# Zero-padded 128-row products in the retention loop, and the 128-row products of a block's outputs put first in the rwkv stage

## The chip, the cores and the metric

The kernel runs on one core of a Trainium2 chip. The metric is the device time of one execution in microseconds, as the median of several runs. Five engines work side by side, each through its own instructions in a fixed order: PE (TensorE, matrix products; PEld is its loading of the stationary operand), DVE (VectorE), ACT (ScalarE), POOL (GpSimd) and SP (SyncE, which issues DMAs here). SBUF is the on-chip memory of 128 rows (partitions); products land in PSUM.

## What is computed

Two blocks of a network run one after the other over 256 tokens of width 1024 in float32. The first block holds a bidirectional retention with 8 heads (64 wide for q and k, 128 for v), a Fourier branch, a gated merge and a convolutional feed-forward part. The second holds an RWKV-7 time mixing with 8 heads of 64, an mLSTM, a gated merge and a PEER layer that fetches 128 expert rows for each token. The parts that the change touches are these:

```python
# retention, first block (o is summed over both directions)
scores = einsum('bhncd,bhnsd->bhncs', qc, kc) * intra_decay
intra = einsum('bhncs,bhnse->bhnce', scores, vc)
inter = einsum('bhncd,nbhde->bhnce', q_dec, s_prev)
o = (intra + inter)
# rwkv, second block
def step(S, inp):
    sa = einsum('bhvk,bhk->bhv', S, -kk_t)
    S = S * w_t[:, :, None, :] + sa[..., None] * b_t[:, :, None, :] + v_t[..., None] * k_t[:, :, None, :]
    return S, einsum('bhvk,bhk->bhv', S, r_t)
```

The kernel computes the retention of all 256 tokens as one chunk: scores times a decay matrix, times v, plus q with a decay times the state `st` that comes from the context. It computes the rwkv recurrence in blocks of 128 tokens, each of two chunks of 64.

## The kernel before

Activations lie transposed, with the width on the 128 rows. A linear layer (`lin`, `lin_units`) streams its float32 weights in units of 512 KB: SP issues the load into one of four buffers `wf`, ACT rounds it to `wh` (line 245), DVE forms the rest `wl` (line 246), three buffers each, and PE makes three products for each 128 rows of contraction (lines 267 to 269 with 256 columns into `psb`, lines 277 to 279 with 512 columns into `psa`).

**The retention loop** (lines 591 to 619) runs over 8 heads. Two heads share the 128 rows of `qt` and `kt`: an even head has rows 0 to 63, an odd one rows 64 to 127 (`rows`). For each head DVE and ACT make the decay matrix `toe` and, for each pair of heads, the decayed q `qd`. Line 606 makes the scores in two halves `pssc`, contracting the head's 64 rows; DVE multiplies them with the decay into `pt` (line 607). Into `pso`, for each of two token blocks, go two products with `v` that contract 128 tokens (line 612) and two with `st` that contract the head's 64 rows (line 614). DVE takes the statistics of the result (lines 617, 618), ACT copies it to `o` (line 619). `st` is filled just before by line 580 (128 rows contracted, 64 outputs in the upper or lower half of the array's columns) and two ACT copies (line 582).

**The outputs of a block in the rwkv stage** (lines 1081 to 1091) follow the chain of the states `zs`. For each of the 8 heads, two products contract 128 tokens (lines 1086 and 1087, 64 outputs), and two contract the head's 64 rows against the states of the two chunks (line 1090, 64 outputs). All go into one PSUM buffer `psy`, and one ACT copy takes it to `yt` (line 1091). This is done twice, for b = 0 and 1.

A float32 product is two passes on PE; in the profile each pass is one instruction, with a load of its own. PSUM has two sets of four buffers; the products here use those of `ps`, the linear layers those of `psd`. Outside the last stage a planner orders each engine's instructions ahead of time, by what is ready and by the order of the program. So products of neighbouring linear layers stand between those of the loop: the gate projection `win[4]`, `win[5]` in the retention loop, `wg2` in the rwkv stage. Named slots for larger tiles come from three size classes, and a freed slot goes to the end of its class's list. The last stage (`experts`) gathers 256 times 1 MB of expert rows by DMAs that POOL issues (line 1472).

Of the kernel before, what the change touches and what calls it, by code (L numbers as in the profile page):

```python
# [19 lines left out]
P = 128  # L20
T = 256
# [3 lines left out]
RH = 8  # L25
# [194 lines left out]
class _Builder:  # L220
# [196 lines left out]
    def block1(self, xt):  # L417
        nc, tc, a, S = self.nc, self.tc, self.a, self.S
# [99 lines left out]
        r = self.rstd(xt)  # L518
# [5 lines left out]
        qt = S([P, 4, T], "qt")  # L524
        f = S([P, 2, 512], "f")

        def fcopy(ps, b):
            nc.scalar.copy(f[:, b], ps)
# [20 lines left out]
        kt = S([P, 4, T], "kt")  # L549
# [15 lines left out]
        v = S([P, 2, D], "v")  # L565
# [8 lines left out]

        st = S([P, 2, 4, P], "st")
        for i in range(2):
            ps = self.ps("psst").rearrange("p (a e) -> p a e", a=4)
            for h in range(RH):
                for b in range(2):
                    nc.tensor.matmul(ps[64 * (h % 2):64 * (h % 2) + 64, h // 2, :], kw[:, i, b, h * 64:(h + 1) * 64],  # L580
                                     vc[:, b, h * P:(h + 1) * P], start=b == 0, stop=b == 1)
            nc.scalar.copy(st[:, i], ps)
        next(rest)
# [7 lines left out]
        for h in range(RH):  # L591
            rows = slice(64 * (h % 2), 64 * (h % 2) + 64)
            if h % 2 == 0:
                qd = self.tmp([P, 2, T], "qd")
# [8 lines left out]
            ps = self.ps("pssc").rearrange("p (a t) -> p a t", a=2)  # L603
            pt = self.tmp([P, 2, T], "pt")
            for j in range(2):
                nc.tensor.matmul(ps[:, j], kt[rows, h // 2, j * P:(j + 1) * P], qt[rows, h // 2, :], start=True, stop=True)
                nc.vector.tensor_mul(pt[:, j], ps[:, j], e[:, 128:384] if j == 0 else e[:, 0:256])
            po = self.ps("pso")
            for b in range(2):
                q = po[:, b * P:(b + 1) * P]  # L610
                for j in range(2):
                    nc.tensor.matmul(q, pt[:, j, b * P:(b + 1) * P], v[:, j, h * P:(h + 1) * P], start=j == 0, stop=False)
                for i in range(2):
                    nc.tensor.matmul(q, qd[rows, i, b * P:(b + 1) * P], st[rows, i, h // 2, :], start=False, stop=i == 1)
            for b in range(2):
# [3 lines left out]
            nc.scalar.copy(o[:, :, h * P:(h + 1) * P], po[:, :256].rearrange("p (b e) -> p b e", b=2))  # L619
        self.dump("o", o)  # L620
        gs = S([P, 2, D], "gs")
        for j in range(2):
# [34 lines left out]

        S.free("v", "kt", "qt", "st")
        rs = cp.tile([P, 2, RH], F32, name="rs8")
# [203 lines left out]
    def rwkv(self, hx, soon, xt, r, C, V):  # L863
# [107 lines left out]
        for b in range(2):  # L971
# [3 lines left out]
            tm = {}  # L975
# [80 lines left out]
            for half in range(2):  # L1056
# [23 lines left out]
                yield  # L1080
            ps = self.ps("psy").rearrange("p (n t) -> p n t", n=4)
            for h in range(RH):
                rows = slice(64 * (h % 2), 64 * (h % 2) + 64)
                hs = slice(h * 64, (h + 1) * 64)
                n = h // 2
                nc.tensor.matmul(ps[rows, n], tm["v"][:, hs], mt(h, 3), start=True, stop=False)
                nc.tensor.matmul(ps[rows, n], u[:, hs], mt(h, 1), start=False, stop=False)
                for half in range(2):
                    tr = slice(64 * half, 64 * half + 64)
                    nc.tensor.matmul(ps[rows, n, tr], zs[2 * b + half][rows, n], kr[rows, n, b, 1, tr], start=False, stop=half == 1)  # L1090
            nc.scalar.copy(yt[:, :, bs], ps)
            S.free("tmz0", *(("tmz1",) if b == 0 else ()), "tmv", "tmq", "rt", "tt", "ktt", "u", "uv")
# [512 lines left out]
```

## Time and profile before

| | |
|---|---|
| median of 3 runs | 1519.98 us (1519.15 to 1525.84) |
| profiled execution | 1517.43 us, its span 1515.7 us |
| PE busy | 1350.3 us (89%) |
| DVE busy | 1047.1 us (69%) |
| ACT busy | 737.7 us (49%) |
| POOL busy | 295.2 us (19%) |
| retention loop | 144.9 to 194.4 us |
| outputs of the two blocks in the rwkv stage | 676.3 to 684.2 and 754.6 to 762.7 us |
| gathering of expert rows | from about 850 us to the end |

The profile is taken from one execution. In the rows of the next section, a product's tile is written as rows contracted times outputs (`64*128` is 64 rows and 128 outputs), then the shape of the moving operand; `x4` means that four such instructions are merged in one row. A product's length holds its way through the array, so that products overlap each other: what counts is the step from one start to the next.

### The profile page before, as it was taken

Reading aid. Unit: us, or ns where it says so; the run is one execution under the profiler, and the core shown is the slowest. Engines: PE = TensorE matmul, PEld = TensorE weight load, DVE = VectorE, ACT = ScalarE, POOL = GpSimd, SP = SyncE. Lnnn points to the kernel's source line nnn. Section 1 sums busy time; section 2 is a strip of 40 time slices with the busy share of each in tenths; the row PEclk is TensorE's granted clock in tenths of the full one; section 3 lists DMA queues with packets and bytes.
Section 4 is the critical chain, followed back from the end, with each engine's and each line's share of the span. In section 5 each row is a group of like instructions: output and inputs, shape, how many; then the busy total and the mean of one; then the engine's idle time right before and its main releaser. Section 6 shows DMA issues by size and latency. Waiting matters only on the chain.

```text
span 1515.7 us, 21089 instructions
## 1 busy us (share of the span) xinstructions
PE 1350.3 (89%) x7496; PEld 969.3 (64%) x7496; DVE 1047.1 (69%) x2095; ACT 737.7 (49%) x1561; POOL 295.2 (19%) x277
## 2 busy tenths in 40 slices
PE   6999999989999999999999779877987798777776
PEld 2788699989999988899889525333532253222222
DVE  6774676867777688755468778678567775867544
ACT  7633454456555586534465454443534444434433
POOL 0000000000000000000000254443444345444331
PEclk9999999999999999999999999999999999999999
DMA  8655376645555444312138599999999999999995
GB/s 289 234 177 176 122 236 214 223 156 186 187 182 183 165 148 133 112 57 84 57 129 282 224 422 419 421 421 421 405 422 421 421 408 422 421 422 420 422 421 237
DMA packets 76568, 413.07 MB, mean 273 GB/s; under 512 B 8640, under 2 KB 8768, under 8 KB 43312
## 3 DMA queue, kind: packets, MB, share of 16 engines
q0 software_dynamic: 38880, 276.59, 44.2%
q1 hardware_dynamic: 37440, 134.88, 26.7%
q8 instruction: 59, 0.97, 0.3%
q14 instruction: 45, 0.37, 0.1%
q10 hardware_dynamic: 144, 0.26, 0.0%
HBM read 410.66 MB, written 1.05 MB: 272 GB/s over the span
## 4 chain that ended last, share of the span: by engine, by line
PE 50%; DMA 19%; DVE 12%; issue 11%; POOL 5%; ACT 4%; POOLq 0%; DVEq 0%; SPq 0%; ACTq 0%
DMA uv<-in_uv_dram,rows 18%; PE psb L267 8%; PE psb L268 8%; PE psb L269 8%; POOL uv L1472 5%; DVE uv L1479 4%; PE acc L1485 2%; PE psa L277 2%; PE psa L279 2%; PE psa L278 2%; PE acc L267 1%; PE acc L269 1%; PE acc L268 1%; ACT wh L245 1%; PE psr L1032 1%
## 5 line engine op out<-in xcount | busy, mean ns | idle before, releaser
L1485 PE MATMUL acc<-uv,dg 128*128 128x512 f32 x1024 | 488.5, 614 | 131.3 <-ACT dg L1483 128.8
L1485 PEld LDWEIGHTS acc<-uv,dg 128*128 128x128 f32 x1024 | 182.1, 191 | 426.7 <-ACT dg L1483 268.2
L1479 DVE CUSTOM_DVE_ANT_0 uv<-uv,hn 128x1024 f32<-128x1024 f32 x256 | 310.2, 1222 | 172.8 <-DMA uv<-in_uv_dram,rows 165.9
L1472 POOL DMA_INDIRECT uv<-in_uv_dram,rows x256 | 283.3, 1107 | 396.0 <-PE acc L1485 264.9
L246 DVE TENSOR_TENSOR wl<-wf,wh 128x1024 fp32r<-128x1024 f32 x213 | 258.3, 1218 | 128.3 <-ACT wh L245 126.8
L245 ACT CAST wh<-wf 128x1024 fp32r<-128x1024 f32 x213 | 222.3, 1046 | 240.5 <-PE psb L268 145.7
L267 PE MATMUL psb<-hxh,wh 128*128 128x256 f32 x960 | 279.3, 291 | 4.2 <-ACT hxh L370 3.4
L268 PE MATMUL psb<-hxl,wh 128*128 128x256 f32 x960 | 273.3, 285 | 0.0
L269 PE MATMUL psb<-hxh,wl 128*128 128x256 f32 x960 | 272.7, 285 | 0.2 <-DVE wl L246 0.2
L1480 ACT ACTIVATE act<-act 128x1 f32<-128x1 f32 x256 | 52.1, 203 | 341.2 <-DVE act L1479 341.1
L267 PEld LDWEIGHTS psb<-hxh,wh 128*128 128x128 f32 x960 | 184.2, 192 | 10.7 <-issue 4.7
L268 PEld LDWEIGHTS psb<-hxl,wh 128*128 128x128 f32 x960 | 184.1, 192 | 3.7 <-issue 2.9
L269 PEld LDWEIGHTS psb<-hxh,wl 128*128 128x128 f32 x960 | 183.8, 192 | 1.0 <-issue 0.3
L1483 ACT ACTIVATE dg<-io,act 128x128 f32<-128x128 f32 x256 | 103.3, 403 | 8.3
L1481 ACT ACTIVATE act<-act,gate 128x1 f32<-128x1 f32 x256 | 76.0, 297 | 8.3
L970 POOL MEMSET mt<- 128x2048 f32 x2 | 3.5, 1804 | 350.8 <-PE psb L268 350.8
L833 POOL DMA_DIRECT2D wq<-in_wq_dram x12 | 6.3, 531 | 260.7 <-PE pstm L982 141.3
L478 DVE SCALAR_TENSOR_TENSOR macc<-wf,cs,macc 128x512 f32<-128x512 f32 x56 | 42.0, 749 | 19.1 <-DMA wf<-in_wmod_dram 18.3
L267 PE MATMUL acc<-fh,wh 128*128 128x256 f32 x176 | 49.5, 281 | 0.0
L268 PE MATMUL acc<-fl,wh 128*128 128x256 f32 x176 | 49.4, 281 | 0.0
L269 PE MATMUL acc<-fh,wl 128*128 128x256 f32 x176 | 49.4, 281 | 0.0
L277 PE MATMUL psa<-wh,hxh 128*128 128x512 f32 x96 | 38.4, 400 | 0.0
(463 smaller groups left out, 2071.2 us busy)
## 6 DMA issues: line engine op xcount, KB each, us to landing
wf<-in_wmod_dram SPq DMA_DIRECT2D x48, 512.0 KB, 4.2
wf<-in_wup_dram SPq DMA_DIRECT2D x44, 512.0 KB, 3.5
wf<-in_win_dram SPq DMA_DIRECT2D x28, 512.0 KB, 4.5
wf<-in_wdn_dram SPq DMA_DIRECT2D x22, 512.0 KB, 3.7
wf<-in_wbg_dram SPq DMA_DIRECT2D x16, 512.0 KB, 4.5
wf<-in_wo_dram SPq DMA_DIRECT2D x16, 512.0 KB, 4.8
wf<-in_wml_dram SPq DMA_DIRECT2D x16, 512.0 KB, 3.4
wf<-in_wg_dram SPq DMA_DIRECT2D x16, 512.0 KB, 3.4
```

Of the source, the lines that this page charges most:

```text
L245: self.nc.scalar.copy(h, src)
L246: self.nc.vector.tensor_sub(l, src, h.bitcast(F32))
L267: nc.tensor.matmul(ps, p, xh[:, k0 + k, :], start=s, stop=False, skip_group_check=True)
L268: nc.tensor.matmul(ps, p, xl[:, k0 + k, :], start=False, stop=False, skip_group_check=True)
L269: nc.tensor.matmul(ps, q, xh[:, k0 + k, :], start=False, stop=e, skip_group_check=True)
L277: nc.tensor.matmul(ps, x, wh[:, k, :n], start=s, stop=False)
L1472: nc.gpsimd.indirect_dma_start(t, None, a["uv"], bass.IndirectOffsetOnAxis(ap=self.rows[b][:, h, k:k + 1], axis=0))
L1479: nc.vector.tensor_tensor_reduce(t[:, :D], t[:, :D], hn[:, b], 1.0, 0.0, ALU.mult, ALU.add, act)
L1480: nc.scalar.activation(act, act, AF.Gelu)
L1481: nc.scalar.activation(act, act, AF.Copy, scale=self.gate[b][:, h, k:k + 1])
L1483: nc.scalar.activation(dg, ident, AF.Copy, scale=act)
L1485: nc.tensor.matmul(acc[b][c], dg, t[:, D + c * 512:D + (c + 1) * 512], start=False, stop=h == PH - 1 and k == TOPK - 1, skip_group_check=True)
```

## The change

In the retention loop, the 64-row products become 128-row products. `qz` holds two copies of `qt`, one with zeros in the lower 64 rows, the other with zeros in the upper ones; POOL writes the zeros and copies the rest. `st` gets a place for each of the 8 heads, with zeros (written by POOL) in the rows of the other head; four ACT copies fill it instead of two. Lines 606 and 614 then contract all 128 rows. `st` moves to a larger slot class, `qz` takes two slots more, and `v`, `kt`, `qt`, `st` and `qz` are released right after the loop.

In the rwkv stage, two PSUM buffers `py` take the even and the odd heads. The two 128-row products of all 8 heads are issued first, then the 64-row products of all heads. The accumulation is opened by the first product in each buffer and closed by the last. Two ACT copies take the two halves to `yt`.

```diff
+        qz = [S([P, 4, T], "qz%d" % i) for i in range(2)]
+        nc.gpsimd.memset(qz[0][64:], 0.0)
+        nc.gpsimd.memset(qz[1][:64], 0.0)
...
-        st = S([P, 2, 4, P], "st")
+        st = S([P, 2, RH, P], "st")
+        nc.gpsimd.memset(st[64:, :, ::2], 0.0)
+        nc.gpsimd.memset(st[:64, :, 1::2], 0.0)
+        for i in range(2):
+            r = slice(64 * i, 64 * i + 64)
+            nc.gpsimd.tensor_copy(qz[i][r], qt[r])
...
-            nc.scalar.copy(st[:, i], ps)
+            for b in range(2):
+                r = slice(64 * b, 64 * b + 64)
+                nc.scalar.copy(st[r, i, b::2], ps[r])
...
-            rows = slice(64 * (h % 2), 64 * (h % 2) + 64)
...
-                nc.tensor.matmul(ps[:, j], kt[rows, h // 2, j * P:(j + 1) * P], qt[rows, h // 2, :], start=True, stop=True)
+                nc.tensor.matmul(ps[:, j], kt[:, h // 2, j * P:(j + 1) * P], qz[h % 2][:, h // 2, :], start=True, stop=True)
...
-                    nc.tensor.matmul(q, qd[rows, i, b * P:(b + 1) * P], st[rows, i, h // 2, :], start=False, stop=i == 1)
+                    nc.tensor.matmul(q, qd[:, i, b * P:(b + 1) * P], st[:, i, h], start=False, stop=i == 1)
...
+        S.free("v", "kt", "qt", "st", "qz0", "qz1")
...
-        S.free("v", "kt", "qt", "st")
...
-            ps = self.ps("psy").rearrange("p (n t) -> p n t", n=4)
+            py = [self.ps("psy").rearrange("p (n t) -> p n t", n=4) for _ in range(2)]
+            at2 = lambda h: (slice(64 * (h % 2), 64 * (h % 2) + 64), h // 2, slice(h * 64, (h + 1) * 64))
             for h in range(RH):
-                rows = slice(64 * (h % 2), 64 * (h % 2) + 64)
-                hs = slice(h * 64, (h + 1) * 64)
-                n = h // 2
-                nc.tensor.matmul(ps[rows, n], tm["v"][:, hs], mt(h, 3), start=True, stop=False)
-                nc.tensor.matmul(ps[rows, n], u[:, hs], mt(h, 1), start=False, stop=False)
+                rows, n, hs = at2(h)
+                nc.tensor.matmul(py[h % 2][rows, n], tm["v"][:, hs], mt(h, 3), start=n == 0, stop=False, skip_group_check=True)
+                nc.tensor.matmul(py[h % 2][rows, n], u[:, hs], mt(h, 1), start=False, stop=False, skip_group_check=True)
+            for h in range(RH):
+                rows, n, hs = at2(h)
                 for half in range(2):
                     tr = slice(64 * half, 64 * half + 64)
-                    nc.tensor.matmul(ps[rows, n, tr], zs[2 * b + half][rows, n], kr[rows, n, b, 1, tr], start=False, stop=half == 1)
-            nc.scalar.copy(yt[:, :, bs], ps)
+                    nc.tensor.matmul(py[h % 2][rows, n, tr], zs[2 * b + half][rows, n], kr[rows, n, b, 1, tr], start=False,
+                                     stop=n == 3 and half == 1, skip_group_check=True)
+            for i in range(2):
+                rows = at2(i)[0]
+                nc.scalar.copy(yt[rows, :, bs], py[i][rows])
```

## Rows read from the trace of the kernel before

**Rows 1.** The page, part 1: busy time, share of span, instructions

```profile
PE 1350.3 (89%) x7496; PEld 969.3 (64%) x7496; DVE 1047.1 (69%) x2095; ACT 737.7 (49%) x1561; POOL 295.2 (19%) x277
```

**Rows 2.** Busy time by stage: retention loop, and the fetching of expert rows

```profile
core 0: us, PE busy (x) PEld busy (x) DVE busy (x) ACT busy (x) POOL busy (x), PEclk, DMA share, GB/s
144.90:194.40 49.50, 49.50 (x235) 34.52 (x235) 32.64 (x94) 18.76 (x31) 1.83 (x3) 1.00 0.40 132
...
849.00:1505.00 656.00, 524.49 (x1368) 223.50 (x1366) 451.63 (x1052) 286.19 (x860) 283.31 (x256) 0.99 1.00 412
```

**Rows 3.** Timeline of PE and PEld, retention loop: start, length, engine, line, operands

```profile
144.89 0.70 PE L606 MATMUL pssc<-qt,kt 64*128 64x256 f32 x2
...
162.22 0.52 PEld L614 LDWEIGHTS pso<-st,qd 64*128 64x128 f32 x4
162.22 0.71 PE L614 MATMUL pso<-st,qd 64*128 64x128 f32 x4
162.86 0.71 PE L612 MATMUL pso<-v,pt 128*128 128x128 f32 x4
163.50 0.71 PE L614 MATMUL pso<-st,qd 64*128 64x128 f32 x4
...
192.41 0.50 PE L277 MATMUL psa<-wh,hxh 128*128 128x512 f32 x1
192.74 0.39 PE L278 MATMUL psa<-wl,hxh 128*128 128x512 f32 x1
192.97 0.40 PE L279 MATMUL psa<-wh,hxl 128*128 128x512 f32 x1
```

**Rows 4.** PE's groups by line and form, 144.89 to 192.4: busy, mean

```profile
L612 PE MATMUL pso<-v,pt 128*128 128x128 f32 x64 | 12.7, 300 | 0.0
L614 PE MATMUL pso<-st,qd 64*128 64x128 f32 x64 | 11.3, 297 | 0.0
L606 PE MATMUL pssc<-qt,kt 64*128 64x256 f32 x32 | 11.1, 428 | 0.0
L279 PE MATMUL psa<-wh,hxl 128*128 128x512 f32 x19 | 8.2, 432 | 0.0
...
L482 PE MATMUL pst<-io,macc 128*128 128x1 f32 x9 | 1.2, 241 | 0.0
```

**Rows 5.** Waits, 144.9 to 194.4: us in total, times, longest

```profile
DVE bs L617 <- PE pso L614: 10.0, 8, 2.4
...
DVE pt L607 <- PE pssc L606: 3.2, 6, 1.5
```

**Rows 6.** PE's timeline in the rwkv stage, one head of block b = 1

```profile
755.60 0.43 PE L1086 MATMUL psy<-mt,tmv 128*64 128x128 f32 x2
...
756.18 0.44 PE L1090 MATMUL psy<-kr,zs 64*64 64x64 f32 x4
756.55 0.43 PE L1086 MATMUL psy<-mt,tmv 128*64 128x128 f32 x2
```

**Rows 7.** PE's timeline: three runs of products that reach only part of the array

```profile
140.21 3.77 PE L580 MATMUL psst<-vc,kw 128*64 128x128 f32 x64
...
671.17 0.68 PE L1077 MATMUL psz<-tmv,tmz 64*64 64x64 f32 x16
...
747.80 0.68 PE L1067 MATMUL psu<-zs,ktt 64*64 64x64 f32 x8
```

**Rows 8.** Single lines, x count: duration ns min/median/max, first and last start

```profile
L970 POOL MEMSET mt<- x2: 1802/1804/1807, 541.0 to 542.7; 128x2048 f32 x2
...
L413 DVE TENSOR_TENSOR qt<-qt,ru x2: 691/692/693, 71.5 to 73.7; 128x512 f32<-128x512 f32 x2
...
L1091 ACT COPY yt<-psy x2: 587/588/589, 684.3 to 762.8; 128x512 f32<-128x512 f32 x2
```

**Rows 9.** Waits of ACT, 194.4 to 250: us in total, times, longest

```profile
ACT wh L245 <- PE psb L268: 20.9, 14, 2.7
```

**Rows 10.** Busy time by stage at 784 us, columns as in rows 2

```profile
784.00:788.00 4.00, 4.00 (x21) 3.96 (x21) 3.99 (x11) 1.93 (x3) 1.75 (x4) 0.57 0.09 14
```

## The prediction

> **What bounds the kernel now.** I read the page first: PE is busy for 89% of the span [rows 1]. That is an average over two very different parts, so the second view was the busy time by stage. From 849 us to the end the core fetches expert rows: all 16 DMA engines are busy (share 1.00, 412 GB/s) and PE waits [rows 2]. That part is as long as its bytes, and it starts when the work before it is done. Everything before 849 us therefore reaches the end one for one, if it lies on the path there. In the retention loop (144.9 to 194.4) PE has no idle time at all, while DVE is busy for 32.64 of 49.50 us and ACT for 18.76 [rows 2]. So PE's in-order stream sets that stage. What follows is fed ahead of PE: between 194 and 250 us ACT waits 20.9 us for PE to give back weight buffers [rows 9]. Time that PE saves in the loop is thus not lost again to the weights behind it.
>
> But "PE busy" does not say that products run at full rate. The third view, PE's timeline, shows it. One 128-column float32 pass follows the other after 0.111 us: four weight loads of L614 take 0.52 us, one takes 0.187, and (0.52 - 0.187) / 3 = 0.111 [rows 3]. Four passes should then take 0.44 us from group to group. They take 0.64 (162.22, 162.86, 163.50), each time the height of the operands goes from 64 to 128 rows or back [rows 3]. The excess is 0.196 us for a change of height.
>
> **Part 1, the retention loop.** The sum over the whole loop checks this. From 144.89 to 192.41 are 47.52 us [rows 3]. In them run 64 passes of L612 and 64 of L614 at 0.111 (14.2 us), 32 of L606 with 256 columns at twice that (7.1), 57 filler passes of the gate projection (19 on each of three lines) at 0.23, the step from 192.74 to 192.97 (13.1), and the small L482 (at most 1.2, taken as 0.8) [rows 3, 4]. Together 35.2; 12.3 us are left. In the timeline the 64-row products stand in 32 groups (16 of L606 in twos, 16 of L614 in fours), each with 128-row products on both sides: 64 changes, 12.3 / 64 = 0.19 us each, the same as from single groups. Hence nothing else of size is hidden there. The change makes every product of the loop 128 rows high and removes all 64: -12.3 to -12.5 us of PE.
>
> What it costs on PE: a 128-row pass takes what a 64-row pass takes (L612 and L614 both go 0.64 us per four with one change, so 0.111 each [rows 3]), so the zeros cost nothing. Here a rule of the Trainium skill speaks against the change: TensorEngine Tiling (Array Packing), Performance Considerations, advises to split the array by rows in two where 64 rows or fewer are contracted, as two such products can then run side by side. The same page, Tiling Modes, says that a change of mode drains the array, which agrees with the 0.196 us. The rows show no overlap to lose: the groups of one head all use the same 64 rows, and the next head's come after 128-row products. What it would be if there were one is the second rival.
>
> What it uncovers: the loop's PE work becomes 49.5 - 12.4 = 37.1 us, and DVE still has 32.6, 88% of it. Most of DVE's idle time now is waiting for the very products that get faster: 10.0 us for the outputs of L614, 3.2 for the scores of L606 [rows 5]. With less slack some of it turns round: the scores' second half goes through DVE (L607) before its product, with one head of lead. The ends are -12.4 (all of it gained) and -8.1, if each of the 8 heads makes PE wait as long as DVE now waits for the scores (3.2 us in 6 waits, 0.53 each: 4.3 in sum). I take -10.8, nearer the first, since PE still has the longer sum. Clearly more is not to be had, as PE waits for nothing else in the loop.
>
> What it adds beside PE. POOL writes zeros and copies. One memset of 2048 columns takes 1.80 us [rows 8], so one of 1024 about 0.9; a copy of 1024 columns is not in the trace, at least 0.9 and, reading as well as writing, perhaps 1.8. qt is complete at 74.4 us (last write starts 73.7) [rows 8], its zeroed copies are first needed at 144.89 [rows 3], and POOL is idle all that time. If the planner puts the copies behind the memsets of st, which wait for the context's last projection, they start near 140.2, when L580 begins [rows 7], and need 2 x 0.9 + 2 x 1.8 = 5.4 us: 0.7 us late. The cost lies between 0 and 1 us; I take 0 as POOL has 70 us for them. st's four copies instead of two (0.59 us each, the form of [rows 8]) end 1.2 us later, but the first product that reads st comes only after the first scores and their DVE step. The earlier release of v, kt, qt, st only renames slots: each later tile gets a slot that was freed as early as before. 0.
>
> **Part 2, the outputs in the rwkv stage.** Per head there are four 128-row passes, then four 64-row ones: 0.95 us (755.60 to 756.55), of which 0.58 and 0.37 [rows 6]. Eight heads make 7.6 us per block, two blocks 15.2. PE does next to nothing else in those stretches. After the change 32 passes of the first kind come in a row. L580 has their very form (128 rows, 64 outputs, 128 columns) and their order (four passes to one half of the array's columns, then four to the other): 64 of them take 3.77 us, 0.058 each [rows 7], half of 0.111, so the two halves run side by side; today the change of height after each head prevents it. Likely 32 x 0.058 = 1.9 us, at most 32 x 0.111 = 3.6. The 32 passes of 64x64 then follow, with neighbouring heads in opposite quarters and in two PSUM banks: 0.058 each where a run stays in one quarter (L1067, (0.68 - 0.27) / 7) and 0.027 where quarters alternate (L1077, (0.68 - 0.27) / 15) [rows 7]: 0.9 to 1.9 us, and I take 1.2, as four passes stay and then change. One change of height is left, 0.2. Likely 3.3 per block, -4.3; bounds 5.7 (-1.9) and 3.0 (-4.6). Two blocks: -8.6, from -3.8 to -9.2.
>
> Beside it: the output goes out in two ACT copies instead of one, +0.59 us each time [rows 8], and two of the four shared PSUM buffers are held instead of one, though for 3 us instead of 8. Queued behind the second copy on ACT are the copies of the next block's transposes, whose products on PE need these buffers. PE has projection products to put in between, so 0, and at most 1 us in sum.
>
> **The sum.** -10.8 - 8.6 = -19.4 us. The profiled execution took 1517.4 us (1.7 outside its span); it would take 1498.0. The median of the runs is 2.6 above it, so the forecast is 1519.98 - 19.4 = 1500.5.
>
> **Rivals.** (1) DVE becomes the bound of the loop and the halves don't overlap: 1520 - 8.1 - 3.8 = 1508. For it: DVE at 88%. Against it: PE's sum is still longer, and L580's rate is measured in this kernel. 12%. (2) The row tiling's overlap is lost. The 64-row passes of the loop are 64 x 0.111 + 32 x 0.222 = 14.2 us; if pairs now ran side by side, padding would give back 7.1: 1507.6. The Trainium skill's page above gives this as the rule. Against it are the equal 0.111 us. 3%. (3) The change doesn't do what it says: the 0.196 us hang on something other than height (the output buffer, a new accumulation) and stay in the loop; only part 2 gains: 1511.4, or 1516 with its lower bound. Against it: changes between buffers at equal height cost no such step (192.74, 192.97 follow at the plain 0.23). 9%. (4) Slower, by the clock. At 784 to 788 us, after products that are only a few rows high, the granted clock averages 0.57, mostly the lower of its two levels (1.2 instead of 2.4 GHz) [rows 10]. If the rwkv stage fell to it for long, because its 64x64 products now stand in one run and PE meets waits that it has not now, each microsecond of PE work would cost one more: past 19.4 us of such work the gain is gone, past 27 the kernel is slower by 0.5%, and 30 us give 1500.5 + 30 = 1530.5. Against it: 1.00 in the loop [rows 2] with the same kinds of products, and a run of 64x64 lasts near 1 us. 4%.
>
> **How the numbers follow.** Forecast 72%, rivals 12, 3, 9 and 4. Predicted 1500.5. The range goes from all bounds at their best (-12.5 - 9.2, and the 2.6 us by which the profiled run beats the median) to between the first and the third rival: 1495 to 1511, leaving out the third in most of its part and the fourth. About 0.5% (7.6 us) can be told from no change: faster is the forecast and the first two rivals, 0.87; same the third, 0.09; slower the fourth, 0.04.
>
> **What would show it.** Part 1: no 64-row form left on L606 and L614, groups of four at 0.44 us in PE's timeline, the loop at 37 to 41 us, and DVE's waits for L614 shrinking while some waits of PE for DVE appear on the second product of L612. Part 2: one run of 32 passes at 0.06 and one of 32 at 0.03 to 0.06, 3 to 4 us from L1086's counterpart to the next product. The DMA-bound part must keep its length and only start earlier. I am wrong if the loop keeps its 49 us with 128-row forms, if DVE fills the time that PE frees, or if the start of the expert stage moves by much less than the two stages shrink.

## The result, and the profile after

The changed kernel was run in three sets, each beside the kernel before on the same chip:

| set | changed kernel, median | kernel before, median | ratio, 95% interval |
|---|---|---|---|
| first | 1504.38 us (1502.32 to 1506.47) | 1520.55 us | 0.9887 [0.9860, 0.9915] |
| second | 1501.55 us (1499.75 to 1506.13) | 1519.99 us | 0.9885 [0.9860, 0.9910] |
| third | 1502.48 us (1501.32 to 1503.21) | 1521.34 us | 0.9872 [0.9856, 0.9889] |

It is faster by 1.1 to 1.3%: 16.2, 18.4 and 18.9 us. The forecast was 1500.5 us, 19.4 us less than before. The time lies within the range. The first profiled execution of the changed kernel took 1506.47 us (span 1504.7), the slowest of its set.

**The retention loop.** PE's timeline answers to [rows 3] (start, length, engine, line, operands; L616, L622 and L624 are the former L606, L612 and L614):

```profile
146.77 0.68 PE L616 MATMUL pssc<-qz,kt 128*128 128x256 f32 x2
...
160.32 0.61 PE L624 MATMUL pso<-st,qd 128*128 128x128 f32 x4
160.77 0.61 PE L622 MATMUL pso<-v,pt 128*128 128x128 f32 x4
161.22 0.61 PE L624 MATMUL pso<-st,qd 128*128 128x128 f32 x4
...
182.96 0.48 PE L277 MATMUL psa<-wh,hxh 128*128 128x512 f32 x1
```

No 64-row form is left. A group of four steps by 0.45 us instead of 0.64. The loop runs from 146.77 to 182.96, 36.19 us instead of 47.52, with the same 57 filler passes of the gate projection inside: 11.33 us less. In two more executions it took 35.47 us (144.56 to 180.03, 143.58 to 179.05), 12.05 less.

The busy time over that loop (columns as in [rows 2]) and four of the waits from 144.9 to 194.4 us (us in total, times, longest) answer to [rows 2, 5]:

```profile
146.77:182.96 36.19, 35.94 (x228) 31.60 (x227) 30.73 (x87) 18.09 (x30) 1.97 (x3) 1.00 0.49 160
```

```profile
DVE pt L617 <- PE pssc L616: 1.1, 1, 1.1
PEld pssc L616 <- DVE pt L617: 0.9, 2, 0.6
...
DVE bs L627 <- PE pso L624: 0.2, 1, 0.2
...
PE pssc L616 <- DVE pt L617: 0.2, 1, 0.2
```

DVE is now busy for 30.73 of 36.19 us, 85%, and still PE's products wait for it only 0.2 us. PE's weight loads wait for it too: 0.9 us ahead of the scores and 0.5 us once ahead of L622. In the two later executions 0.5 us of this is left, and the loop is 0.72 us shorter. DVE's wait for the scores fell from 3.2 to 1.1 us, and that for the outputs (L614 before, L624 now) from 10.0 to 0.2 us.

**The outputs in the rwkv stage.** PE's timeline of the two blocks, which answers to [rows 6] (L1096, L1097 and L1102 are the former L1086, L1087 and L1090):

```profile
670.16 0.43 PE L1096 MATMUL psy<-mt,tmv 128*64 128x128 f32 x2
...
670.75 0.67 PE L1087 MATMUL psz<-u,tmz 64*64 64x64 f32 x14
671.35 0.45 PE L1096 MATMUL psy<-mt,tmv 128*64 128x128 f32 x4
...
673.24 1.20 PE L1102 MATMUL psy<-kr,zs 64*64 64x64 f32 x32
674.37 0.66 PE L992 MATMUL pstm<-io,bz 128*128 128x128 f32 x4
```

```profile
744.83 0.43 PE L1096 MATMUL psy<-mt,tmv 128*64 128x128 f32 x2
...
746.72 1.14 PE L1102 MATMUL psy<-kr,zs 64*64 64x64 f32 x16
747.79 0.49 PE L1258 MATMUL psmo<-va,mpt 128*128 128x129 f32 x2
748.21 0.43 PE L1096 MATMUL psy<-mt,tmv 128*64 128x128 f32 x2
...
750.10 1.14 PE L1102 MATMUL psy<-kr,zs 64*64 64x64 f32 x16
751.17 0.39 PE L268 MATMUL psb<-hxl,wh 128*128 128x256 f32 x1
```

Within one buffer the passes of L1096 and L1097 take turns by twos, so the `x4` of b = 0 are taken to be two passes of an even head and two of an odd one; the first head's four passes came alone. From 671.35 to 673.24, 28 passes take 1.89 us, 0.068 each; 32 passes of 64x64 take 1.13. The 14 passes of L1087 (the former L1077) in between take 0.60. The block goes from 7.90 us (676.26 to 684.16 before, products of other lines inside in both) to 4.21: 3.7 less. In b = 1 the heads of one buffer, the even ones, all come first, then those of the other. ACT copies the first half of the outputs out before the second run of 64x64 passes begins:

```profile
748.39 0.57 ACT L1106 COPY yt<-psy 64x512 f32<-64x512 f32 x1
```

In each run 16 passes take 1.89 us (744.83 to 746.72 in the first), 0.118 each with the change of height behind them; a pair of passes steps by 0.22, so 0.109 each without it. The 16 passes of 64x64 behind each take 1.07 us, 0.055 each without the change, where b = 0 has 0.029. The block goes from 8.04 us (754.64 to 762.68) to 6.34: 1.7 less.

**The rest.** The stage that fetches expert rows keeps its length: its products run from 858.0 to 1508.8 us before, from 847.8 to 1497.9 after. It still runs at the rate of its DMAs (columns as in [rows 2]):

```profile
849.00:1494.00 645.00, 534.72 (x1351) 227.20 (x1350) 445.45 (x1033) 279.52 (x850) 276.06 (x249) 0.97 1.00 415
```

The three stretches give 11.3 + 3.7 + 1.7 = 16.7 us. The two first profiles differ by only 11.0 (1515.7 to 1504.7 us). Part of what is missing is lost ahead of the loop, which starts at 146.77 instead of 144.89. The rest is taken up with the run of the changed kernel again, below.

### The profile page after: what moved, and what is told of

The parts are those of the page before. It is cut to its first block, busy times and chain, and to the rows that moved or that the text cites. A ratio compares the mean times of both kernels' runs of the same rounds, so it can differ in the third digit from the quotient of the medians.

```text
span 1504.7 us, 21103 instructions
## 1 busy us (share of the span) xinstructions
PE 1352.3 (90%) x7496; PEld 975.6 (65%) x7496; DVE 1048.2 (70%) x2095; ACT 739.0 (49%) x1566; POOL 301.3 (20%) x283
## 4 chain that ended last, share of the span: by engine, by line
PE 51%; DMA 19%; DVE 11%; issue 9%; POOL 5%; ACT 4%; POOLq 0%; SPq 0%; DVEq 0%; ACTq 0%
DMA uv<-in_uv_dram,rows 17%; PE psb L267 9%; PE psb L268 9%; PE psb L269 9%; POOL uv L1487 5%; DVE uv L1494 4%; PE acc L1500 3%; DMA wf<-in_wmod_dram 2%; PE psa L277 2%; PE psa L279 2%; PE psa L278 2%; PE acc L267 1%; PE acc L269 1%; PE acc L268 1%; PE psr L1042 1%
## 5 line engine op out<-in xcount | busy, mean ns | idle before, releaser
L1500 PE MATMUL acc<-uv,dg 128*128 128x512 f32 x1024 | 501.9, 630 | 116.8 <-ACT dg L1498 114.2
L1500 PEld LDWEIGHTS acc<-uv,dg 128*128 128x128 f32 x1024 | 188.1, 196 | 419.7 <-ACT dg L1498 251.3
L267 PE MATMUL acc<-fh,wh 128*128 128x256 f32 x176 | 49.5, 281 | 0.0
```

What stands on the lines that cost most here:

```text
L267: nc.tensor.matmul(ps, p, xh[:, k0 + k, :], start=s, stop=False, skip_group_check=True)
L1500: nc.tensor.matmul(acc[b][c], dg, t[:, D + c * 512:D + (c + 1) * 512], start=False, stop=h == PH - 1 and k == TOPK - 1, skip_group_check=True)
```

## The experiments

The theory: a change between 64-row and 128-row products costs PE 0.196 us; the loop gains by the changes that go, and the output blocks gain where the two column halves of the array run side by side. The rivals are those of the prediction, and one more for b = 1: its order comes from the PSUM buffers that are free. None of these kernels leaves out a part of the computation.

### e1_loop_only: part 1 alone

The rwkv outputs as in the kernel before, the retention loop as in the changed one.

```diff
-            py = [self.ps("psy").rearrange("p (n t) -> p n t", n=4) for _ in range(2)]
+            ps = self.ps("psy").rearrange("p (n t) -> p n t", n=4)
...
```

> Part 1 alone: the retention loop with zero-padded operands, the outputs of the rwkv stage as before. Theory (a change between 64-row and 128-row products costs PE 0.196 us, and 64 of them go): the loop takes the 36.2 us that it takes in the changed kernel instead of 47.5, and the time falls by 11.3 us (ends 9 and 13), whatever the rwkv stage does. Rival (part of the gain comes out of the rwkv stage or the earlier release of the retention buffers): the fall is under 8 us or the loop is not near 36 us. Rival (POOL's zeros and copies delay the first scores): the loop begins over 1 us later than in the kernel before.

Measured: 1507.67 us against 1519.19, ratio 0.9924 [0.9897, 0.9950], 11.5 us less. PE's timeline at the two ends of the loop:

```profile
143.35 0.68 PE L616 MATMUL pssc<-qz,kt 128*128 128x256 f32 x2
...
179.40 0.48 PE L277 MATMUL psa<-wh,hxh 128*128 128x512 f32 x1
```

The loop takes 36.05 us, 11.5 less than before. What it loses in length is what the time loses, and it starts no later than before. Both rivals fall.

### e2_outputs_only: part 2 alone

The retention loop as in the kernel before, the rwkv outputs as in the changed one; the lines are shown against the changed kernel.

```diff
...
-                nc.tensor.matmul(ps[:, j], kt[:, h // 2, j * P:(j + 1) * P], qz[h % 2][:, h // 2, :], start=True, stop=True)
+                nc.tensor.matmul(ps[:, j], kt[rows, h // 2, j * P:(j + 1) * P], qt[rows, h // 2, :], start=True, stop=True)
...
-                    nc.tensor.matmul(q, qd[:, i, b * P:(b + 1) * P], st[:, i, h], start=False, stop=i == 1)
+                    nc.tensor.matmul(q, qd[rows, i, b * P:(b + 1) * P], st[rows, i, h // 2, :], start=False, stop=i == 1)
...
```

> Part 2 alone: the outputs of the rwkv stage in the new order with two buffers, the retention loop as before. The prediction gave it 8.6 us (4.3 for each block). Theory now (PE's column halves run side by side only where neighbouring products alternate between them; in block b = 1 the planner puts all even heads ahead of the odd ones, because the second buffer is still held by the mLSTM head's products): 4.3 for b = 0 and 1.7 for b = 1, so the time falls by 6.0 us, and the two stretches take 3.6 and 6.3 us. Rival (the order in b = 1 comes from part 1, by the shifted due times): b = 1 alternates here, both take 3.6 us, and the time falls by 8.6.

Measured: 1513.88 us against 1519.19, ratio 0.9963 [0.9943, 0.9982], 5.3 us less. The loop takes 47.52 us as before. Block b = 0 takes 4.20 us (678.08 to 682.28), which is the expected 3.6 and the 0.6 of the products of L1077 in between. PE's timeline shows b = 1 split again:

```profile
752.75 0.43 PE L1086 MATMUL psy<-mt,tmv 128*64 128x128 f32 x2
...
754.64 1.14 PE L1092 MATMUL psy<-kr,zs 64*64 64x64 f32 x16
...
759.10 0.39 PE L268 MATMUL psb<-hxl,wh 128*128 128x256 f32 x1
```

6.35 us. So the order of b = 1 is not brought by part 1, and part 2 is worth 3.7 + 1.7 = 5.4 us in its stretches and 5.3 in the time. The two parts add up: 11.5 + 5.3 = 16.8.

### e3_scores_only: half of the changes of height

From the kernel before, with padded queries only; POOL fills `qz`, and the buffers are released right after the loop, as in the changed kernel.

```diff
...
-                nc.tensor.matmul(ps[:, j], kt[rows, h // 2, j * P:(j + 1) * P], qt[rows, h // 2, :], start=True, stop=True)
+                nc.tensor.matmul(ps[:, j], kt[:, h // 2, j * P:(j + 1) * P], qz[h % 2][:, h // 2, :], start=True, stop=True)
...
```

> From the kernel before, only the scores of the retention loop get zero-padded queries; the products with st keep 64 rows and the rwkv outputs stay as before. 16 groups of 64-row products are left in place of 32, so 32 changes of height in place of 64. Theory (0.196 us for each change of height): the loop falls by 32 x 0.196 = 6.3 us less what DVE gives back, 47.5 to about 41.5, and the time by 6. Rival 3 of the prediction in its general form (the 0.196 us hang on the change of output buffer or on a new accumulation): buffers and accumulations are those of before, so the loop stays near 47.5. Rival (PE's overlap of 64-row products): the padded scores, 32 passes of 256 columns, would become longer, not shorter, and the fall would be under 3 us.

Measured: 1512.54 us against 1519.19, ratio 0.9951 [0.9936, 0.9966], 6.7 us less. PE's timeline at the two ends:

```profile
147.63 0.68 PE L613 MATMUL pssc<-qz,kt 128*128 128x256 f32 x2
...
189.13 0.50 PE L277 MATMUL psa<-wh,hxh 128*128 128x512 f32 x1
```

41.50 us with 57 fillers and 32 changes, as expected: 6.0 us for 32 changes, 0.19 each. Padding the queries changed neither which PSUM buffer a product goes to nor where an accumulation begins, so the third rival falls.

### e5_grouped: fewer changes, no zeros

From the kernel before. For each head the products with `v` of both token blocks come first, then those with `st`.

```diff
...
+            for j in range(2):
+                for b in range(2):
+                    q = po[:, b * P:(b + 1) * P]
+                    nc.tensor.matmul(q, pt[:, j, b * P:(b + 1) * P], v[:, j, h * P:(h + 1) * P], start=j == 0 and b == 0, stop=False, skip_group_check=True)
...
-                for j in range(2):
-                    nc.tensor.matmul(q, pt[:, j, b * P:(b + 1) * P], v[:, j, h * P:(h + 1) * P], start=j == 0, stop=False)
...
```

> The kernel before, without any zeros: in the retention loop the products of a head with v come first for both token blocks, then all with st, so that the 64-row products stand in 24 runs instead of 32. Operands, heights and work are the same; only the order changes: 48 changes of height in place of 64. Theory (0.196 us for each change): the loop falls by 16 x 0.196 = 3.1 us, to about 44.4, and the time by 3.1. Rival (the 128-row form itself, not the change, is what gains): the loop stays at 47.5.

Measured: 1517.55 us against 1519.99, ratio 0.9984 [0.9965, 1.0004], 2.4 us less; the interval just holds 1, so the time alone does not show it. PE's timeline does, here of one head:

```profile
183.01 0.71 PE L612 MATMUL pso<-v,pt 128*128 128x128 f32 x4
183.66 1.16 PE L616 MATMUL pso<-st,qd 64*128 64x128 f32 x8
184.74 0.50 PE L277 MATMUL psa<-wh,hxh 128*128 128x512 f32 x1
```

Eight passes of 64 rows take 1.08 us: 8 x 0.111 and one change of 0.196. The loop takes 46.08 us (144.87 to 190.95) with 64 fillers; less 7 of them at 0.231 it is 44.46, and 44.4 was expected. Without a single zero, 16 changes less are worth 3.1 us of the loop. It is the change that costs, not the 64-row form.

### e6_pairs: can 64-row products run side by side?

From the kernel before. The scores of a pair of heads alternate between the upper and the lower 64 rows.

```diff
...
+            if h % 2 == 0:
+                pss = [self.ps("pssc").rearrange("p (a t) -> p a t", a=2) for _ in range(2)]
+                for j in range(2):
+                    for y in range(2):
+                        ry = slice(64 * y, 64 * y + 64)
+                        nc.tensor.matmul(pss[y][:, j], kt[ry, h // 2, j * P:(j + 1) * P], qt[ry, h // 2, :], start=True, stop=True)
...
-            ps = self.ps("pssc").rearrange("p (a t) -> p a t", a=2)
+            ps = pss[h % 2]
...
-                nc.tensor.matmul(ps[:, j], kt[rows, h // 2, j * P:(j + 1) * P], qt[rows, h // 2, :], start=True, stop=True)
...
```

> The kernel before, without any zeros: the scores of the two heads of a pair are issued alternately, one on the upper 64 rows of the array, one on the lower, into two output buffers. This gives the row-tiling rival of the prediction its best case. Rival (64-row products in opposite halves run side by side): four passes of 256 columns take about 0.43 us plus one change, half of the four times 0.222 = 0.89 us in series, so the loop falls by 8 x 0.45 = 3.6 us more than the saved changes alone. Theory (they run in series): the four passes take 0.89 us, and the loop falls only by the changes of height that go, 8 to 16 of them at 0.196 (1.6 to 3.1 us).

Measured: 1514.56 us against 1519.99, ratio 0.9970 [0.9959, 0.9982], 5.4 us less. PE's timeline, first pair and a later one:

```profile
143.61 1.13 PE L603 MATMUL pssc<-qt,kt 64*128 64x256 f32 x8
144.68 0.49 PE L277 MATMUL psa<-wh,hxh 128*128 128x512 f32 x1
...
161.48 0.70 PE L603 MATMUL pssc<-qt,kt 64*128 64x256 f32 x2
162.11 0.49 PE L617 MATMUL pso<-v,pt 128*128 128x128 f32 x2
```

Here the theory was wrong and the rival right. The eight alternating passes of 256 columns take 1.07 us with one change, so 0.109 each (four products are eight passes; the expectation's 0.43 and 0.89 counted half of them). The two passes of one head alone take 0.63 with one change, 0.217 each. Opposite row halves do run side by side, if neighbouring products alternate between them.

The loop takes 42.26 us with 58 fillers, 5.5 less than before at equal fillers. 24 changes go, not the 8 to 16 expected, because later scores joined a group of `st` products: 4.7 us. Side by side gives 0.9 in the first pair and about 0.5 in each later one, some 2.3. About 1.5 us are given back. The profile shows 0.6 of it as PE waiting for `pt`; the rest is not traced.

### e4_heads and e11_heads_long: block b = 1 alternating

The changed kernel, with the second mLSTM head handed to the planner after b = 1's outputs instead of ahead of them.

```diff
-HEADS = (27, 28, 30, 32)
+HEADS = (27, 29, 30, 32)
```

> The changed kernel with the second mLSTM head handed to the planner after block b = 1's outputs instead of before them, so that both output buffers are free when the outputs begin and the even and odd heads alternate there. Theory (alternating halves run side by side, one after the other in one half does not): b = 1's stretch falls from 6.3 us to the 3.6 us of b = 0, and the time by 2.5 us against the changed kernel (some 13.5 to 19 us below the kernel before, as that compares at 16.1 now in medians). Rival (b = 1 is slow for another reason, such as waits for ACT's copies): the stretch stays above 5 us. Rival (the moved head costs elsewhere what the stretch saves): the stretch falls but the time doesn't.

> The kernel with the moved mLSTM head again, in more rounds: its output stretch was 3.0 us shorter than in the changed kernel, but its median was not. Theory (the 3 us reach the end, less 1.6 us of new waits behind the outputs; the rest was hidden by stretches at the lower clock, which lie elsewhere in each execution): 1.5 to 3 us below the changed kernel in this call. Rival (the moved head gives all of it back): within 0.7 us of the changed kernel.

PE's timeline of b = 1 in the first of the two:

```profile
736.17 0.45 PE L1096 MATMUL psy<-mt,tmv 128*64 128x128 f32 x4
...
738.12 1.20 PE L1102 MATMUL psy<-kr,zs 64*64 64x64 f32 x32
739.25 0.39 PE L269 MATMUL psb<-hxh,wl 128*128 128x256 f32 x1
```

The heads alternate and the block takes 3.08 us instead of 6.34. Of the difference 0.4 us are two passes of the mLSTM head (747.79 to 748.21), which stood between the two runs and are gone from there. 32 passes take 1.95 us with one change, 0.055 each. So the alternation decides, as the theory says; that before the second buffer was held by the mLSTM head is what the edit suggests, though no row names the buffer.

The times: 1501.75 us against 1519.19 (0.9884 [0.9858, 0.9910]), and in more rounds 1501.19 against 1521.34 (0.9869 [0.9850, 0.9888]), where the changed kernel had 1502.48 (0.9872). That is 1.3 us less, of the 3.3 us that the block gained: under the 1.5 to 3 of the theory, above the 0.7 of the rival, and within the spread of its five runs (1498.39 to 1503.99 us). PE's waits from 735 to 800 us in the longer run (us in total, times, longest):

```profile
PE psb L269 <- DVE wl L246: 0.7, 1, 0.7
PE psms L1251 <- DVE yt L1130: 0.5, 1, 0.5
PE psgn L1129 <- DVE rsg L1125: 0.4, 1, 0.4
PE psb L268 <- DVE yml L246: 0.2, 1, 0.2
PE psb L268 <- DVE ml L246: 0.2, 1, 0.2
```

2.0 us, 1.6 more than the changed kernel has there in its two later executions (0.4). And in both executions with the moved head the granted clock is 0.91 from 760 to 780 us, where two of the three executions of the changed kernel have 1.00: about 20 x 0.09 = 1.8 us. The two together would give back what the block gained. But the clock is 0.91 there with part 1 alone too, where no head is moved, so it is not shown that the moved head lowers it. What is shown is that the stretch falls; how much of it reaches the end stays open.

### e7_more_groups: the same kind of order elsewhere in the rwkv stage

The kernel with the moved head, and in each block eight products with 64 outputs after eight with 128, not one by one.

```diff
...
+                nc.tensor.matmul(pm[:, hs], mt(h, 2), tm["v"][:, hs], start=True, stop=True)
+            for h in range(RH):
+                hs = slice(h * 64, (h + 1) * 64)
                 nc.tensor.matmul(ps[64 * (h % 2):64 * (h % 2) + 64, h // 2], tm["q"][:, hs], rt[:, h], start=True, stop=True)
-                nc.tensor.matmul(pm[:, hs], mt(h, 2), tm["v"][:, hs], start=True, stop=True)
...
```

> The kernel with the moved mLSTM head, and besides, in each block of the rwkv stage, eight products with 64 outputs in a run and then eight with 128 outputs, which alternate one by one in the changed kernel. Theory (a change of the array's column split costs like a change of height, about 0.14 us as read from that stage): up to 2 x 14 changes go, 4 us less than with the moved head alone at most, 2 us likely as other products stand between. Rival (that stage waits for DVE or ACT there, not for PE): no difference to the moved head alone within 1.5 us.

Measured: 1498.24 us against 1519.99, ratio 0.9852 [0.9832, 0.9872]; the changed kernel in the same set has 1501.55. PE's timeline, first with the moved head alone, then grouped:

```profile
719.33 0.43 PE L1055 MATMUL psk<-rt,tmq 128*64 128x128 f32 x2
719.70 0.43 PE L1056 MATMUL psm<-tmv,mt 128*128 128x64 f32 x2
```

```profile
717.61 1.90 PE L1055 MATMUL psm<-tmv,mt 128*128 128x64 f32 x16
719.43 1.09 PE L1058 MATMUL psk<-rt,tmq 128*64 128x128 f32 x16
720.46 1.77 PE L1064 MATMUL psu<-u,rt 128*128 128x64 f32 x14
```

One by one, every two passes take 0.363 us on average (719.33 to 719.70 is one such step). In groups they take 1.82 / 16 = 0.114 and 1.03 / 16 = 0.064 each. So a change between 128 and 64 outputs costs about 0.363 - 0.222 = 0.14 us, and the grouped 64-output passes run two side by side. From the outputs of b = 0 to those of b = 1 it is 67.56 us (665.18 to 732.74) instead of 70.73 (665.44 to 736.17), with 199 passes of the projection inside in both: 3.2 less. The time is 3.0 to 3.5 us below the two medians with the moved head alone (1501.75 and 1501.19), which are of other sets; the intervals of their ratios overlap.

### e8_after_again and e10_after_long: the changed kernel again

> The changed kernel once more, unedited, to see what two executions of the same program differ by. Theory: the stretches of lower granted clock fall at other places than in the first profile (there 45 to 55, 315 to 325, 600 to 610, 770 to 780 us), so they are no part of the change; the retention loop takes 36.2 us and the outputs 3.6 and 6.3 again. Rival (the change causes them): they lie at the same places and take the same few us again.

> The changed kernel unedited, on the same chip as the next two, as their measure. Expected: 17 to 18 us below the kernel before (16.7 from the stretches of the two parts: 11.3 for the loop, 3.7 and 1.7 for the output blocks).

The times stand in the first table; the third set, 18.9 us below the kernel before, is a little more than the 17 to 18 expected. The loop took 35.47 us in both, 0.7 less than expected, b = 1 split again (6.34 and 6.35 us), and b = 0 took 4.20 and 4.21. The span was 1498.8 us in the first of the two and 1500.8 in the second, against 1504.7 in the first profile of the same program. Busy time and granted clock in two stretches (columns as in [rows 2]), first in the first profile of the changed kernel, then in its second (e8_after_again):

```profile
300.00:340.00 40.00, 36.07 (x271) 34.87 (x270) 27.59 (x46) 22.80 (x36) 0.00 (x0) 0.91 0.46 142
...
760.00:800.00 40.00, 40.00 (x297) 37.97 (x297) 33.59 (x73) 25.27 (x43) 4.73 (x9) 0.91 0.68 241
```

```profile
300.00:340.00 40.00, 35.94 (x276) 34.67 (x275) 28.66 (x45) 21.47 (x34) 0.00 (x0) 0.96 0.45 142
...
760.00:800.00 40.00, 39.62 (x318) 37.65 (x317) 37.79 (x75) 26.31 (x44) 5.77 (x11) 1.00 0.81 290
```

The kernel before has 0.96 in both. From 20 to 60 us, ahead of the loop, the clock averages 0.87 in the first profile and 0.91 in the second and in the kernel before, and there the loop starts late (146.77 against 144.56 in the second). So the first profile of the changed kernel lost more time in all three stretches to a lower clock than the second, of the same program: by these shares about 40 x 0.04, 40 x 0.05 and 40 x 0.09, in sum some 7 us. Most of the shortfall of that profile (11.0 of 16.7 us) is thus no effect of the change; from before to the second profile the span falls by 16.9, to the third by 14.9. Theory and rival of the expectation are each right in part. The low stretch from 770 to 780 us is not there again (0.66, then 1.00 twice); the one from 600 to 610 is, in all three profiles (0.83, 0.89, 0.83). From 590 to 620 us the clock averages 0.94 in all three and 1.00 before, but 1.00 again in two kernels that hold the whole change (the moved head, the grouped products). What sets it there stays open.

### e9_side_by_side and e12_side_long: both row halves, no zeros

The grouped kernel with `qt` and `st` as before. The two heads of a pair go together, and their 64-row products alternate between the row halves.

```diff
...
+                    for y, r in enumerate(half):
+                        nc.tensor.matmul(po[y][:, b * P:(b + 1) * P], qd[r, i, b * P:(b + 1) * P], st[r, i, g, :],
+                                         start=False, stop=b == 1 and i == 1, skip_group_check=True)
...
```

> The kernel with the grouped rwkv products, but its retention loop without zeros: the two heads of a pair go together, their 64-row scores and 64-row products with st alternating between the upper and the lower half of the array, a pair's products with st followed directly by the next pair's scores. 64-row products stand in 5 runs, so 10 changes of height are left in place of none (0 with zeros) and 64 (before). Theory as it stands after the run with paired scores (opposite halves run side by side at 0.109 us for 256 columns): PE needs 7.1 us for the products with v, 3.5 for the scores, 3.6 for those with st, 2.0 for 10 changes, 13.1 for 57 fillers and 0.8, in sum 30.1 us in place of 36.2. Of these 6 us all come back if DVE (32 us of its own in the loop) has other fillers to hide behind, and 3 if PE waits for it; so 3 to 6 us below the kernel with grouped products. Rival (with st, whose outputs go on in the accumulation that v began, the halves don't overlap): st takes 7.1, and 2.5 us come back at most.

> The fastest kernel so far again, beside the changed kernel: both heads of a pair side by side on the row halves, without zeros, and the grouped rwkv products. Expected from the earlier calls: 5 to 7 us below the changed kernel, 22 to 25 below the kernel before. Rival (its lead was chance): under 3 us below the changed kernel.

Measured: 1495.70 us against 1519.74, ratio 0.9835 [0.9814, 0.9856]; then 1496.58 against 1521.34, ratio 0.9827 [0.9809, 0.9844], with the changed kernel at 1502.48 (0.9872 [0.9856, 0.9889]) in the same set. It beats the kernel before and the changed one, the latter by 5.9 us, which holds the moved head and the grouped products too. PE's timeline of one pair, and PE's wait in the loop:

```profile
146.44 2.05 PE L617 MATMUL pso<-v,pt 128*128 128x128 f32 x16 [0.27 <-DVE pt L611]
148.42 1.16 PE L622 MATMUL pso<-st,qd 64*128 64x128 f32 x16
149.41 1.03 PE L601 MATMUL pssc<-qt,kt 64*128 64x256 f32 x8
```

```profile
PE pso L617 <- DVE pt L611: 2.5, 4, 0.8
```

The 16 passes with `st` take 0.99 us, 0.062 a pass instead of 0.111, although they go on in accumulations that `v` began. The rival falls. The loop from 144.60 to 166.40 holds only 11 fillers. What it gains is read from its start to the first product of the next layer, which has the same work in each kernel, all 96 filler passes with it. Two such ends, first of the grouped kernel (its loop starts at 147.67), then of this one (144.60):

```profile
192.13 0.28 PE L267 MATMUL psb<-hxh,wh 128*128 128x256 f32 x1
```

```profile
186.98 0.28 PE L267 MATMUL psb<-hxh,wh 128*128 128x256 f32 x1
```

That is 44.46 us with zeros and 42.38 without, 2.1 less; the changed kernel again has 44.42 in both executions, the kernel before 56.51, this kernel's second execution 42.42. The 2.5 us of waits for DVE are most of what is missing to the 6 us put for PE's work: now DVE sets part of the pace. The time is 2.5 us below that of the grouped kernel by medians, less than the 3 to 6 expected; those medians are of two sets, and the two intervals overlap, so the lead over padding rests on the stretch.

## Why the prediction was right, and where not

**What bounds the kernel: right.** Time taken from PE's stream ahead of 849 us reached the end, about one for one: 11.5 us of loop gave 11.5 us of time (part 1 alone), 5.4 us of output blocks 5.3 (part 2 alone), and the expert stage only started earlier. For the moved head, where the block gained 3.3 us and the median 1.3, it is not shown.

**Part 1, the price of a change of height: right.** 64 changes at 0.196 us were to give 12.4 us of PE; 11.3 to 12.05 were seen. Half of the changes gave 6.0 (scores alone), a quarter of them, by order alone, 3.1.

**What it uncovers: too dear by a little.** The middle between -12.4 and -8.1 assumed that PE would wait for DVE's scores. Its products wait 0.2 us, its weight loads 1.4 in the first execution and 0.5 in the later ones. The prediction put -10.8, the loop gave -11.3 and twice -12.05. Its 49.5 and 37.1 us of PE work are those of 144.9 to 194.4 us, with 2 us of fillers behind the loop's end at 192.41; the loop itself had 47.52.

**What it adds beside PE: right.** POOL's two copies take 1.18 us each, within the bounds 0.9 to 1.8, and no wait of PE for POOL appears; the loop of part 1 alone starts at 143.35 us, earlier than before.

**Part 2: the mis-sized term.** It was put at -4.3 for each block and gave -3.7 and -1.7, in sum -5.4 instead of -8.6, within the bounds -3.8 to -9.2. The step that failed is "Likely 32 x 0.058 = 1.9 us", taken from L580 for both blocks. L580 changes to the other column half after every four passes. Block b = 1 does not: its even heads all come first, and its passes take 0.109, which was the upper bound. The prediction saw that two of four shared PSUM buffers would be held, and asked only which later copies this delays, with the answer 0. It didn't ask whether both buffers would be free when the block begins, and so in which order the planner could put its heads; that it is the buffer is suggested by the moved mLSTM head, with which the block takes 3.08 us, and not traced. The second size, 1.2 us for the 64x64 passes, was right in b = 0 (1.13 with its change); in b = 1 the two runs took 1.07 each.

**The sum.** -11.3 to -12.05 and -5.4, that is -16.7 to -17.5, against -19.4; the three sets show -16.2, -18.4 and -18.9. The sum came out nearer than its second part, because the first gave 0.5 to 1.3 us more than was put for it: that much is luck.

**The rivals.** DVE did not become the bound (first rival), but its second half came true in one block: the halves did not overlap in b = 1. The second rival, the lost row overlap, was refused for the right reason: the kernel before had no overlap to lose, as its rows showed. But the overlap itself exists, which the prediction left out as a way to gain. The rule of the Trainium skill (TensorEngine Tiling (Array Packing), Performance Considerations) to split the array by rows where 64 rows or fewer are contracted agrees with the runs: alternating products took 0.109 us per 256 columns instead of 0.217. How it compares with padding hangs on the changes of height that are left: with 40 of them (paired scores) the loop fell by 5.5 us, less than with zeros; with 10 it fell by 2.1 more than with zeros. The third rival (the cost hangs on something else) fell with the padded scores and the regrouped order. The rows named against it, 192.74 and 192.97, go on in one `psa` buffer and show no change of buffer; the loop has such a change at equal height elsewhere, from L278 into `psa` at 148.42 to L612 into `pso` at 148.66, and it steps by the plain 0.24. The fourth did not appear: the granted clock in the rwkv stage of the changed kernel is 1.00 from 650 to 755 us in two executions and 0.98 in the third.

**What would have shown it.** Groups of four at 0.44 us: 0.45. Loop at 37 to 41 us: this was taken from the 49.5 us, which become 38.2 and 37.5; the loop itself takes 36.2 and 35.5. DVE's waits for the outputs shrank as announced, from 10.0 to 0.2 us; the waits of PE on L612's second product came to one of 0.5 us in its weight loads in the first execution. One run of 32 passes at 0.06, then one of 32: in b = 0 only.

## What to carry to other kernels

Look in PE's timeline for the step between neighbouring products whose operands have another height or another number of outputs: here each such change cost 0.196 us (height) or 0.14 us (outputs), more than a pass of 128 columns (0.111). Grouping products of one shape, or padding with zeros, removes the changes; alternating between the two halves of the array within a group makes them nearly twice as fast. In this loop that beat padding by 2.1 us, once groups of 8 to 24 passes had left 10 changes of 64. Whether a planner issues that order can depend on what else it has placed, as the moved head showed, so this has to be read from the order that it builds, for each place where the code runs.

## What the runs showed of the hardware that was not expected

Two 64-row products in opposite row halves run side by side in float32, also when they go on in accumulations begun by 128-row products: 0.109 us for 256 columns (alone 0.217), 0.062 for 128 (alone 0.111). Column halves behave alike: 128-row passes with 64 outputs take 0.055 to 0.068 us where the halves alternate, 0.109 where a run stays in one half. The same program can differ by 6 us of its span from one execution to the next (1498.8, 1504.7), with the granted clock lower in three stretches of the longer one, so a difference of two profiles is read stage by stage.
